# Starting every on-chip tile of a fp32 two-block network on a multiple of 64 or 128 bytes

## The chip, the core and the metric

The kernel runs on one core of a Trainium2 chip. The metric is the device time of one execution in microseconds. The kernel is timed several times and the median counts; the profile is one further execution, recorded by the hardware profiler.

## What is computed

The reference is a network on 256 tokens of 1024 features, all in fp32. Its first block adds to the input a pair of linear-attention mixers (RWKV-7 and GLA) and then a mixture of 32 experts, two of them for each token. Its second block has two layers, each made of a feed-forward half, a mixer (two attentions and a Fourier branch, each gated) and another feed-forward half, with scales and shifts that come from a condition vector; it takes the output of the first block as one stream of tokens and a given context as another. Cut to what matters here:

```
x = x + concat(rwkv7(rmsnorm(x) @ w_in), gla(...)) @ w_out        # block 1
x = x + sum over 2 of 32 experts of (silu(h @ w_gate) * (h @ w_up)) @ w_down
for each of 2 layers:                                             # block 2, x and context
    x = x + 0.5 * gate * ffn(rmsnorm(x) * scale + shift)
    x = x + gate * mixer(rmsnorm(x) * scale + shift, keys of the context)
    x = x + 0.5 * gate * ffn(rmsnorm(x) * scale + shift)
```

Nearly all of the arithmetic is products of a weight matrix with the 256 tokens.

## The kernel before

Features lie on the 128 partitions of the on-chip memory (SBUF) and the 256 tokens lie along a partition, so one row of a tile of tokens is 256 fp32 numbers, 1024 bytes. A weight comes in chunks of eight 128x128 tiles. A chunk goes through four steps. SyncE issues a DMA of 128x1024 numbers into one of eight buffers named `raw` (or into further ones, named `room`, while they exist; line 313). ScalarE rounds it to the format that TensorE multiplies in one pass, into `whi` (line 319). VectorE subtracts that from the chunk, into `wlo` (line 320). TensorE then makes three matmuls for each 128x128 tile, in `mm3`: `whi` by the tokens' high part (line 334), `whi` by the tokens' low part (line 335), and `wlo` by the tokens' high part (line 336). Each loads 128x128 weights and moves 128x256 numbers of tokens past them. The next three for the same output add to the same bank of PSUM.

The tokens' operands are pairs of tiles, too. `norm_split` (line 453) writes `hnh` and `hnl`: for each of the 8 groups of 128 features VectorE scales x into a small tile `hnt` of which there are two (line 463), ScalarE adds the shift and rounds into `hnh` (line 468), and VectorE takes the difference into `hnl` (line 469). The feed-forward's inner values are `h0` and `h1` (lines 328 and 329), the branches' are `yh` and `yl`. In some norms the operand is made before the norm is known; then it is `xs0` and `xs1`, rows of 256 numbers and 2 more for the shift (lines 373 to 377).

The letter at the end of a name is the chain that the tile belongs to. Chain x is block 1's mixers and runs until about 447 us. Chain c is the context's way through block 2; it runs from there to 1640 us, with the experts of block 1 (tiles that end in m, products `bm`) between its matmuls. Chain z is the main tokens' way through block 2; it has the chip to itself from 1712 us to the end. The chains' tiles lie at different addresses: long-lived tiles at the left end of a partition, the chains' own ones packed from the right end or behind the left ones.

The order of the work on TensorE and SyncE is written out by the emitting code: generators yield steps, and `_run`, `_zip` and `_merge` choose by an internal clock which goes next. VectorE, ScalarE and GpSimd are ordered by the scheduler of the tile layer, which follows buffers as they come free. The tile layer packs tiles at multiples of 32 bytes.

Of the kernel before, what the change touches and what calls it, by code (L numbers as in the profile page):

```python
# [10 lines left out]
F32 = mybir.dt.float32  # L11
# [8 lines left out]
T = 256  # L20
# [5 lines left out]
HD = 64  # L26


# ----------------------------------------------------------------- host layout
def _tiles(w, cols):  # L30
    """[K, n] -> column tiles in the order of `cols` (lists of 128 column indices), each as K/128 tiles."""
    K = w.shape[0]
    return [w[k * 128:(k + 1) * 128, c] for c in cols for k in range(K // 128)]


def _chunks(tiles):
    """List of [128, 128] tiles -> [n / 16, 128, 16 * 128], zero filled."""
    n = -(-len(tiles) // 16) * 16
    a = np.zeros((n, 128, 128), np.float32)
    for i, t in enumerate(tiles):  # L40
        a[i, :, :t.shape[1]] = t
    return np.ascontiguousarray(a.reshape(n // 16, 16, 128, 128).transpose(0, 2, 1, 3).reshape(n // 16, 128, 2048))


def _cols(v):
    """[n] -> [128, n / 128]."""
    return np.asarray(v, np.float32).reshape(-1, 128).T
# [153 lines left out]
# ----------------------------------------------------------------- the chip's program  # L201
class _Chain:
    """What a chain of the program works with: its tiles in SBUF and its banks of PSUM."""
# [9 lines left out]
    def hold(self):  # L213
        """A bank that stays while others come and go; two at a time."""
        return self.ps.tile([128, 512], F32, tag="h" + self.name, name="h" + self.name, bufs=2)
# [4 lines left out]
    @contextmanager  # L220
    def scope(self, name):
        """A chain whose tiles last as long as the scope."""
        with self.pool(name=name + self.name, bufs=1) as sb:
            yield self.sub(sb)
# [6 lines left out]
class _Net:  # L231
# [7 lines left out]
    def open(self, cpool, rpool, nraw):  # L239
# [8 lines left out]
        self.selT = cpool.tile([128, 512], F32R, name="selT")  # L248

    def splits(self, ch, pool, n):  # L250
        """The pool that holds the split weights of the chain from here on, and its buffers."""
# [37 lines left out]
    # -- weights  # L289
    def arrival(self):  # L290
        """When the next weights would be there, by the clock of the emission."""
# [4 lines left out]
    def room(self, pool, n):  # L296
        """More room for weights that are on their way."""
# [28 lines left out]
    def split_act(self, hi, lo, src):  # L326
        """hi + lo = src, for operands of matrix products."""
# [3 lines left out]
    def mm3(self, out, w, x, first, last, **kw):  # L331
        """out += w.T @ x with both split."""
# [5 lines left out]
    # -- small arithmetic  # L338
    def rsqrt(self, ch, ms, n, eps, tag="rs", op=OP.add):
        """1 / sqrt(ms + eps) on [128, n], in SBUF; with op max, 1 / sqrt(max(ms, eps))."""  # L340
# [13 lines left out]
    def sumsq(self, ch, x, k, nxt=None, eng=None):  # L354
        """Adds the squares of x, the k-th of KD, to the chain's sums: one of all but the last, and the last. With
        nxt, the scale and shift that the norm takes, x by the scale is split ahead of it, the shift beside it."""
# [15 lines left out]
        if k == 0:  # L372
            top.xs = [top.tile([128, KD, T + 2], f"xs{i}", F32R) for i in range(2)]
            self.split_act(*(t[:, :, T:] for t in top.xs), shift[:, :, None].to_broadcast([128, KD, 2]))
# [4 lines left out]
    def early(self, ch, xs, w, tiles, banks):  # L379
        """Products of the first tiles of a weight with what the norm hasn't scaled yet, its shift's beside it."""  # L380
        for o in tiles:
            b = ch.bank()
            banks.append(b)
            for k in range(KD):
                self.mm3(b[:, :T + 2], w.get(o + k), (xs[0][:, k], xs[1][:, k]), k == 0, k == KD - 1)
# [3 lines left out]
    def norm_early(self, ch, x, scale, shift, w, tiles):  # L389
        """norm_split, and what early gives meanwhile: banks, that times the rows of 1 / rms are products, up to a  # L390
        shift by feature in their column T."""
# [10 lines left out]
    def scaled(self, ch, b, rs):  # L402
        """A bank of norm_early times rs, and its shift, in SBUF."""
# [5 lines left out]
    def rstd(self, ch, x, w1=0.7, w2=2.2):  # L409
        """x [128, KD, T], features on partitions: 1 / rms over the features, on all partitions, [128, T] in PSUM."""  # L410
# [5 lines left out]
    def rstd_cols(self, ch, x, w1=0.7, w2=2.2):  # L416
        """1 / rms of the tokens of x, [128 tokens, 2]."""
# [25 lines left out]
    def spread(self, ch, y):  # L443
        """[128 tokens, 2] -> the value of each token on all partitions, [128, T] in PSUM."""
# [8 lines left out]
    def norm_split(self, ch, x, scale, shift, rs=None):  # L453
        """rms norm of x, times scale, plus shift, as split operands [128, KD, T]; 1 / rms into rs."""
# [6 lines left out]
        for k in range(KD):  # L461
            t = ch.tile([128, T], "hnt", bufs=2)
# [11 lines left out]
    # -- block 1  # L474
    def rows(self, b, j, x, n):
        """Means over the heads of x, tile j of n, into the bank b (with unrows)."""
        self.nc.tensor.matmul(b[32 * j:32 * j + 32, :T], self.c("sel")[:, :32], x, start=True, stop=True)

    def parted(self, ch, rs):
        """Values by row as operands of unrows: the high parts in 8 rows of 32, the low parts in the next 8."""  # L480
# [6 lines left out]
    def unrows(self, out, j, st, n=0):  # L487
        """The rows of st for tile j + 4 n on the partitions of its heads."""
# [3 lines left out]
    def head_rsqrt(self, ch, sqs, eps, op):  # L492
        """1 / rms over the heads of 4 tiles, from their squares: [8 heads' high parts, 8 low parts; T], by head_rows."""
# [22 lines left out]
    def mixers(self, ch):  # L516
        """RWKV-7 and GLA of the norm of the input; the input plus their output projection into self.x."""
# [93 lines left out]
    def rwkv(self, ch, sh, lora, yg):  # L611
# [3 lines left out]
        left = self.tc.tile_pool  # L615
# [41 lines left out]
    def until(self, n):  # L657
        """Waits for the mixers of block 1 to have come to their n-th stage."""
# [3 lines left out]
    def beside(self, ch, sh, lora, yg, wo, x, bonus, gate):  # L662
        """What the solve of RWKV-7 doesn't give: its bonus and gate, in place of v and r, and GLA's output projection."""
# [191 lines left out]
    def blocks_out(self, lq, n):  # L855
        """The 32 x 32 blocks on the diagonals of one direction, to where they come back from a block to a partition."""
# [4 lines left out]
    def invert(self, k, ld, kk):  # L861
        """Inverses of the blocks on the diagonals, a block in each partition; in the room of k, ld and kk."""
# [22 lines left out]
    def solve(self, ch, tt, lu, lq, xab, xx):  # L885
        """The solve of RWKV-7 by triangles of 32 x 32; what it gives is added to the latter half of self.x."""
# [5 lines left out]
        def out(j, g):  # L892
            """The part of the output that comes from the first or second 128 tokens to be solved."""
# [14 lines left out]
        def correct(g, corr, todo):  # L908
            """What triangles of u add to those of the m-th after them."""
# [8 lines left out]
        def right(g):  # L918
            """Banks with the right sides of the first or second 128 tokens to be solved."""
# [59 lines left out]
    def rwkv_out(self, ch, bonus, gate, yh, yl):  # L979
        """The group norm of RWKV-7's output, its bonus and its gate, as split operands."""  # L980
# [138 lines left out]
    def route(self, ch, x):  # L1119
        """The router's choices for the tokens of x, and its norm by token (scaled once the tokens have partitions)."""  # L1120
# [46 lines left out]
        def first_max(f, n):  # L1167
            """The index of the first maximum over the last axis, and the maximum."""
# [63 lines left out]
        # assignments beyond an expert's 32 slots go to blocks of 32 of their own  # L1232
# [45 lines left out]
    def swiglu_rows(self, ch, bg, bu, n):  # L1278
        """silu(gate) * up of n rows of 512, and its transpose [128, 4, n]."""
# [14 lines left out]
    def moe(self, ch, x, load, loads):  # L1294
        """x += experts; 4 experts of 32 slots at a time."""
# [69 lines left out]
    def moe_over(self, ch_of, x):  # L1365
        """x += what the assignments beyond 32 of an expert add, a block of 32 of them at a time."""
# [58 lines left out]
    # -- block 2  # L1425
    def silu_c(self, ch):
        """silu of both conditions as stationary operands [128, KD, 32] (columns 0, 1; zeros beyond)."""
# [3 lines left out]
        for m, name in enumerate(("c", "c_ctx")):  # L1431
            t = ch.tile([128, KD], "silc", bufs=2)
            u = ch.tile([128, KD], "silu", bufs=2)
# [4 lines left out]
    def ada(self, ch, l):  # L1438
        """Modulation vectors of layer l: {0: for x, 1: for ctx} -> [128, 72], and what the norms take of them."""
# [4 lines left out]
        m2 = [self.cp.tile([128, 72], F32, name=f"mod{l}{m}") for m in range(2)]  # L1444
# [25 lines left out]
        for m in range(2):  # L1470
            mm = m2[m].rearrange("p (n k) -> p n k", k=KD)
            a = self.cp.tile([128, 3, KD], F32, name=f"nsc{l}{m}")
# [3 lines left out]
            g = self.cp.tile([128, 3, KD], F32, name=f"gsc{l}{m}")  # L1476
# [6 lines left out]
    def lam(self, ch, l):  # L1483
        """-lambda of layer l on all partitions, [128, 1]."""
        nc = self.nc
        lv = self.v(f"lam{l}")
        p = ch.tile([128, 2], "lamp")
# [3 lines left out]
        e = ch.tile([128, 2], "lame")  # L1491
        nc.scalar.activation(e, b[:, :2], AF.Exp)
        qg = self.cp.tile([128, 4], F32, name=f"qkg{l}")
# [3 lines left out]
        nl = self.cp.tile([128, 1], F32, name=f"nlam{l}")  # L1497
        li = 0.8 - 0.6 * math.exp(-0.3 * l)
        nc.vector.scalar_tensor_tensor(nl, e[:, 1:2], li, e[:, 0:1], op0=OP.subtract, op1=OP.subtract)
        gs = self.cp.tile([128, 1], F32, name=f"subg{l}")  # L1500
# [79 lines left out]
    def project(self, ch, hn, l, rope, y, w, first, full=True):  # L1580
        """Queries, keys and values of the tokens, and the operands of the Fourier branch into y."""
# [77 lines left out]
    def rotate(self, ch, qk, norm, rs, l, rope):  # L1659
        """The norm of queries and keys, and their rotation."""  # L1660
# [21 lines left out]
    def fourier(self, ch, uc, y):  # L1682
        """The operands of the Fourier branch into y."""
# [20 lines left out]
    def attend(self, ch, kind, q, keys, y, l=None, room=None):  # L1704
        """Attention of the queries q on the keys, a pair of heads (kind a) or of maps (kind b) at a time, into y. With
        room, a pair of [128, KD, T] tiles, queries and keys are split there."""
# [11 lines left out]
        def prepare(j):  # L1718
            """The operands of the scores of pair j: the queries', and each keys'."""
# [106 lines left out]
    def mixer(self, ch, x, mod, l, rope, other=None, keep=None, full=True, nxt=None):  # L1826
        """The mixer of block 2: `other` gives keys of other tokens, ahead of the own ones; `keep` stores the own."""
# [8 lines left out]
        with ch.scope("macc") if full else nullcontext(ch) as ca:  # L1836
            acc = ca.tile([128, KD, T], "macc") if full else None
            with ch.scope("mix") as cm:
# [6 lines left out]
                if full:  # L1845
                    keys = keys + [r]
                    room = None if first is None else [ch.top.tile([128, KD, T + 2], f"xs{i}", F32R) for i in range(2)]
# [23 lines left out]
    def gate(self, b, hn, wb, o):  # L1871
        """The gate of a branch into the first half of the bank b, its weights from the o-th tile on."""
# [5 lines left out]
    def gates(self, ch, hn, wb, th):  # L1878
        """tanh of half the last branch's first gates."""
# [293 lines left out]
```

## Time and profile before

| | us |
|---|---|
| median of 3 runs | 2986.49 (2985.42 to 2990.33) |
| span of the profiled execution, first to last instruction | 2977.6 |
| TensorE busy in it | 2856.5 (96%) |
| VectorE busy | 1781.8 (60%) |
| ScalarE busy | 1235.6 (41%) |
| GpSimd busy | 179.3 (6%) |
| mean busy share of the 16 DMA engines in 40 slices | between 0.2 and 0.9 |

For the profiled execution the trace gives its span alone; the runs lie 7.8 to 12.7 us above it, which is what lies before the first and after the last recorded instruction. In the rows a matmul of 128x256 numbers shows some 0.28 us from its start to its end, although the next one starts about 0.12 us after it: matmuls follow each other through a pipeline. The speed of a stream of matmuls is therefore read from the distance between starts and not from the busy time. PE means TensorE, PEld its loading of weights, DVE VectorE, ACT ScalarE, POOL GpSimd and SP SyncE.

### The profile page before, as it was taken

What the parts mean: (1) busy time and instruction counts of PE and PEld (TensorE: products, weight loads), DVE (VectorE), ACT (ScalarE), POOL (GpSimd) and SP (SyncE); (2) the same over time, 40 slices, a digit from 0 to 9 for tenths busy, and PEclk for the clock granted to TensorE, in tenths of its full rate; (3) what the DMA queues carried; (4) which work ended last, traced back from release to release, by engine and by line L of the source; (5) the groups of instructions that cost most, each with busy time, mean ns of one, the idle gap of its engine ahead of it and who ended that gap; (6) DMA issues with size and microseconds to landing.
All of it is one profiled execution on the core that took longest, in us unless ns stands there. A gap on an engine that the chain in (4) does not pass through costs nothing. (4 is left out here: it accounts for less than half of the span.)

```text
span 2977.6 us, 55032 instructions
## 1 busy us (share of the span) xinstructions
PE 2856.5 (96%) x22394; PEld 2419.8 (81%) x22394; DVE 1781.8 (60%) x3517; ACT 1235.6 (41%) x2071; POOL 179.3 (6%) x207
## 2 busy tenths in 40 slices
PE   8999777999999999999999899999999999999999
PEld 5756457787756778877887699989999999899999
DVE  4565565454534454545545766767776767766865
ACT  3321133333324333333333454556554545465543
POOL 0110110000000010000000000010200000101100
PEclk9999888999999999999999999999999999999999
DMA  8755857887787888897988565523556556424564
GB/s 316 251 177 176 292 212 197 299 290 280 235 274 271 303 281 317 291 339 285 336 294 312 183 197 193 192 82 107 163 191 196 181 196 201 139 86 137 169 194 132
DMA packets 198897, 667.47 MB, mean 224 GB/s; under 512 B 36850, under 2 KB 37874, under 8 KB 198002
## 3 DMA queue, kind: packets, MB, share of 16 engines
q1 hardware_dynamic: 180144, 656.04, 63.8%
q10 hardware_dynamic: 18498, 7.90, 1.3%
q8 instruction: 176, 2.88, 0.4%
q14 instruction: 79, 0.65, 0.1%
HBM read 658.05 MB, written 5.80 MB: 223 GB/s over the span
## 5 line engine op out<-in xcount | busy, mean ns | idle before, releaser
L320 DVE TENSOR_TENSOR wlo<-raw,whi 128x1024 fp32r<-128x1024 f32 x623 | 767.7, 1233 | 493.9 <-ACT whi L319 481.4
L319 ACT CAST whi<-raw 128x1024 fp32r<-128x1024 f32 x631 | 661.6, 1050 | 772.4 <-issue 278.6
L334 PE MATMUL bz<-hnhz,whi 128*128 128x256 f32 x1920 | 539.8, 281 | 0.7 <-ACT hnhz L328 0.7
L335 PE MATMUL bz<-hnlz,whi 128*128 128x256 f32 x1920 | 532.7, 277 | 4.2 <-DVE hnlz L329 4.2
L336 PE MATMUL bz<-hnhz,wlo 128*128 128x256 f32 x1920 | 532.0, 277 | 0.6 <-DVE wlo L320 0.6
L334 PE MATMUL bc<-hnhc,whi 128*128 128x256 f32 x1504 | 440.6, 293 | 13.0 <-ACT whi L319 12.2
L335 PE MATMUL bc<-hnlc,whi 128*128 128x256 f32 x1504 | 428.5, 285 | 4.8 <-DVE hnlc L469 2.8
L336 PE MATMUL bc<-hnhc,wlo 128*128 128x256 f32 x1504 | 427.7, 284 | 4.8 <-DVE wlo L320 4.8
L334 PEld LDWEIGHTS bz<-hnhz,whi 128*128 128x128 f32 x1920 | 361.4, 188 | 9.6 <-issue 5.7
L334 PEld LDWEIGHTS bc<-hnhc,whi 128*128 128x128 f32 x1504 | 289.6, 193 | 94.0 <-issue 37.2
L335 PEld LDWEIGHTS bz<-hnlz,whi 128*128 128x128 f32 x1920 | 361.4, 188 | 5.5 <-DVE hnlz L329 5.4
L336 PEld LDWEIGHTS bz<-hnhz,wlo 128*128 128x128 f32 x1920 | 361.5, 188 | 0.8 <-DVE wlo L320 0.8
L335 PEld LDWEIGHTS bc<-hnlc,whi 128*128 128x128 f32 x1504 | 290.1, 193 | 7.5 <-DVE hnlc L469 5.9
L336 PEld LDWEIGHTS bc<-hnhc,wlo 128*128 128x128 f32 x1504 | 289.7, 193 | 6.4 <-DVE wlo L320 6.4
L334 PE MATMUL bz<-h0z,whi 128*128 128x256 f32 x704 | 194.3, 276 | 0.0
L335 PE MATMUL bz<-h1z,whi 128*128 128x256 f32 x704 | 194.3, 276 | 0.0
L336 PE MATMUL bz<-h0z,wlo 128*128 128x256 f32 x704 | 194.3, 276 | 0.0
L334 PE MATMUL bc<-h0c,whi 128*128 128x256 f32 x528 | 154.2, 292 | 0.6 <-ACT h0c L328 0.6
L335 PE MATMUL bc<-h1c,whi 128*128 128x256 f32 x528 | 150.1, 284 | 0.9 <-DVE h1c L329 0.9
L336 PE MATMUL bc<-h0c,wlo 128*128 128x256 f32 x528 | 149.8, 284 | 0.0
L1337 PE MATMUL bm<-raw,mxm 128*32 128x512 f32 x752 | 147.3, 606 | 1.1 <-DMA raw<-moe_gu 1.1
L320 DVE TENSOR_TENSOR wlo<-room,whi 128x1024 fp32r<-128x1024 f32 x75 | 91.7, 1224 | 86.9 <-ACT whi L319 77.8
(702 smaller groups left out, 5328.1 us busy)
## 6 DMA issues: line engine op xcount, KB each, us to landing
raw<-wi SPq DMA_DIRECT2D x263, 512.0 KB, 4.7
raw<-moe_gu SPq DMA_DIRECT2D x188, 512.0 KB, 7.1
raw<-wada SPq DMA_DIRECT2D x144, 512.0 KB, 4.8
raw<-wo SPq DMA_DIRECT2D x124, 512.0 KB, 4.5
raw<-wbr SPq DMA_DIRECT2D x108, 512.0 KB, 3.7
raw<-win SPq DMA_DIRECT2D x104, 512.0 KB, 5.0
raw<-moe_dn SPq DMA_DIRECT2D x103, 512.0 KB, 5.9
room<-moe_gu SPq DMA_DIRECT2D x68, 512.0 KB, 8.9
```

Of the source, the lines that this page charges most:

```text
L319: self.nc.scalar.copy(hi, src)
L320: eng.tensor_tensor(lo, src, hi.bitcast(F32), op=OP.subtract)
L334: mm(out, w[0], x[0], start=first, stop=False, **kw)
L335: mm(out, w[0], x[1], start=False, stop=False, **kw)
L336: mm(out, w[1], x[0], start=False, stop=last, **kw)
L1337: mm(b[32 * j:32 * j + 32], xt[:, k, 32 * j:32 * j + 32], r[:, j % 2 * 512:j % 2 * 512 + 512], start=(k == 0), stop=(k == KD - 1))
```

## The change

A wrapper, `_Pool`, stands between the kernel and the pools of SBUF. It rounds the size of each tile up, to 16 numbers (64 bytes) if it has no more than 16 on a partition and otherwise to a multiple of 32 numbers (128 bytes), and hands out the first part of it. Pools of PSUM and of DRAM are as before. The many small vectors (modulation, its derived scales, and the like) become slices of one tile, `small`. The rows of `xs0` and `xs1` become 272 numbers (1088 bytes) where they were 258 (1032 bytes). A tile of 96 bytes, `edge`, is put at the right end of the partition so that what is packed from there begins on a multiple of 128. `norm_split`'s temporary comes from the chain's general pool `w` (three buffers) and no longer from `hnt` (two). The rest of the difference takes away comments.

```diff
+XS = T + 16
+class _Pool:
+    def tile(self, shape, dt=F32, **kw):
+        n = math.prod(shape[1:])
+        full = 16 if n <= 16 else -(-n // 32) * 32
+        if full == n:
+            return self.pool.tile(shape, dt, **kw)
+        t = self.pool.tile([shape[0], full], dt, **kw)[:, :n]
+        if len(shape) == 2:
+            return t
+        names = "abcd"[:len(shape) - 1]
+        return t.rearrange(f"p ({' '.join(names)}) -> p {' '.join(names)}", **dict(zip(names, shape[1:])))
+def _pools(tc):
+    @contextmanager
+    def pool(name, bufs=1, **kw):
+        with tc.tile_pool(name=name, bufs=bufs, **kw) as p:
+            yield p if "space" in kw else _Pool(p)
+    return pool
...
+        self.small, self.taken = cpool.tile([128, 544], F32, name="small"), 0
+    def take(self, n):
+        self.taken += n
+        return self.small[:, self.taken - n:self.taken]
...
-            top.xs = [top.tile([128, KD, T + 2], f"xs{i}", F32R) for i in range(2)]
-            self.split_act(*(t[:, :, T:] for t in top.xs), shift[:, :, None].to_broadcast([128, KD, 2]))
+            top.xs = [top.tile([128, KD, XS], f"xs{i}", F32R) for i in range(2)]
+            self.split_act(*(t[:, :, T:T + 2] for t in top.xs), shift[:, :, None].to_broadcast([128, KD, 2]))
...
-                self.mm3(b[:, :T + 2], w.get(o + k), (xs[0][:, k], xs[1][:, k]), k == 0, k == KD - 1)
+                self.mm3(b[:, :T + 2], w.get(o + k), (xs[0][:, k, :T + 2], xs[1][:, k, :T + 2]), k == 0, k == KD - 1)
...
         for k in range(KD):
-            t = ch.tile([128, T], "hnt", bufs=2)
+            t = ch.tile([128, T], "w", bufs=ch.nw)
...
-        left = self.tc.tile_pool
+        left = _pools(self.tc)
...
-        m2 = [self.cp.tile([128, 72], F32, name=f"mod{l}{m}") for m in range(2)]
+        m2 = [self.take(72) for m in range(2)]
...
-            a = self.cp.tile([128, 3, KD], F32, name=f"nsc{l}{m}")
+            a = self.take(3 * KD).rearrange("p (i k) -> p i k", i=3)
...
-    pool = tc.tile_pool
+    pool = _pools(tc)
...
+    ctx.enter_context(tc.tile_pool(name="edge", bufs=1, side="right")).tile([128, 24], F32, name="edge")
     rp = ctx.enter_context(pool(name="raw", bufs=1))
     net.open(base, rp, 8)
+    net.cw, net.nover = net.take(4), net.take(1)[0:1].bitcast(I32)
```

Where the tiles start, in both programs as they are built: the remainder of the byte address in a partition by 128 (a second buffer of the same tile, or the next row, is a multiple of 128 further on, but for the rows of xs).

| tile | before | after |
|---|---|---|
| raw | 32 | 0 |
| whi, wlo (all chains) | 32 | 0 |
| hnhx, hnhc, h0c | 32 | 0 |
| hnhz, h0z | 96 | 0 |
| yhz | 0 | 64 |
| xs0z, first row and further ones | 96, then 8 more each | 0 or 64 |
| mstm, mxm (experts' sums) | 64 | 64 |
| mylm (experts' sums) | 96 | 0 |
| x | 0 | 0 |

TensorE and SyncE run the same instructions in the same order before and after, under other names. ScalarE, VectorE and GpSimd change places at the norms. On ScalarE, at the second norm of chain z (`hnhz` is the normalised tokens' high part, `hntz` and `wz` the temporary, `mod` and `small` the shift), before:

```order
L458 COPY hnrz<-bz 128x256
L319 CAST whi<-raw 128x1024 x2
L468 ACTIVATE hnhz<-hntz,mod_325 128x256 x2
L319 CAST whi<-raw 128x1024
L468 ACTIVATE hnhz<-hntz,mod_325 128x256 x2
L319 CAST whi<-raw 128x1024
```

and after, where lines 353, 492 and 502 are the former lines 319, 458 and 468:

```order
L492 COPY hnrz<-bz 128x256
L353 CAST whi<-raw 128x1024 x2
L502 ACTIVATE hnhz<-wz,small 128x256 x3
L353 CAST whi<-raw 128x1024
L502 ACTIVATE hnhz<-wz,small 128x256 x3
L353 CAST whi<-raw 128x1024
```

The eight activations come in groups of three instead of two between the casts of the weights, with a cast less among them. On VectorE at the same norm, before:

```order
L320 TENSOR_TENSOR wlo<-raw,whi 128x1024
L463 SCALAR_TENSOR_TENSOR hntz<-x,nsc_2509,bz 128x256 x2
L320 TENSOR_TENSOR wlo<-raw,whi 128x1024
L469 SCALAR_TENSOR_TENSOR hnlz<-hntz,mod_325,hnhz 128x256 x2
L463 SCALAR_TENSOR_TENSOR hntz<-x,nsc_2509,bz 128x256 x2
L320 TENSOR_TENSOR wlo<-raw,whi 128x1024
```

and after, where lines 354, 497 and 503 are the former lines 320, 463 and 469:

```order
L354 TENSOR_TENSOR wlo<-raw,whi 128x1024
L497 SCALAR_TENSOR_TENSOR wz<-x,small,bz 128x256 x3
L354 TENSOR_TENSOR wlo<-raw,whi 128x1024
L503 SCALAR_TENSOR_TENSOR hnlz<-wz,small,hnhz 128x256 x3
L497 SCALAR_TENSOR_TENSOR wz<-x,small,bz 128x256 x3
L503 SCALAR_TENSOR_TENSOR hnlz<-wz,small,hnhz 128x256 x3
L497 SCALAR_TENSOR_TENSOR wz<-x,small,bz 128x256 x2
```

Here, too, three of a kind stand together, and fewer subtractions for the weights come between them.

## Rows read from the trace of the kernel before

**Rows 1.** The page's part on the engines: busy time, share, instructions.

```profile
PE 2856.5 (96%) x22394; PEld 2419.8 (81%) x22394; DVE 1781.8 (60%) x3517; ACT 1235.6 (41%) x2071; POOL 179.3 (6%) x207
```

**Rows 2.** Stretches: length; PE, PEld, DVE, ACT, POOL busy (count); clock; DMA share; GB/s.

```profile
471.60:474.60 3.00, 3.00 (x16) 3.00 (x15) 2.76 (x21) 1.34 (x4) 0.00 (x0) 0.50 0.76 287
520.00:1640.00 1120.00, 1095.74 (x8285) 867.44 (x8284) 555.74 (x943) 406.98 (x649) 37.83 (x40) 1.00 0.82 294
1265.48:1339.90 74.42, 73.63 (x584) 58.45 (x583) 34.63 (x46) 27.71 (x39) 2.17 (x3) 1.00 0.90 339
1712.00:2977.60 1265.60, 1242.82 (x10369) 1195.80 (x10367) 877.01 (x1512) 650.22 (x1076) 83.79 (x88) 1.00 0.50 162
```

**Rows 3.** Groups by line: busy us, mean ns of one, idle before and what ended it.

```profile
L320 DVE TENSOR_TENSOR wlo<-raw,whi 128x1024 fp32r<-128x1024 f32 x623 | 767.7, 1233 | 493.9 <-ACT whi L319 481.4
L319 ACT CAST whi<-raw 128x1024 fp32r<-128x1024 f32 x631 | 661.6, 1050 | 772.4 <-issue 278.6
L334 PE MATMUL bz<-hnhz,whi 128*128 128x256 f32 x1920 | 539.8, 281 | 0.7 <-ACT hnhz L328 0.7
L334 PE MATMUL bc<-hnhc,whi 128*128 128x256 f32 x1504 | 440.6, 293 | 13.0 <-ACT whi L319 12.2
...
L334 PE MATMUL bz<-h0z,whi 128*128 128x256 f32 x704 | 194.3, 276 | 0.0
...
L334 PE MATMUL bc<-h0c,whi 128*128 128x256 f32 x528 | 154.2, 292 | 0.6 <-ACT h0c L328 0.6
```

**Rows 4.** Timeline of PE, chain z, 195 matmuls without a break (first, last).

```profile
2240.05 0.28 PE L335 MATMUL bz<-hnlz,whi 128*128 128x256 f32 x1
...
2262.03 0.28 PE L334 MATMUL bz<-hnhz,whi 128*128 128x256 f32 x1
```

**Rows 5.** Timeline of PE, chain c, 65 matmuls without a break (first, last).

```profile
591.35 0.28 PE L335 MATMUL bc<-h1c,whi 128*128 128x256 f32 x1
...
599.02 0.28 PE L336 MATMUL bc<-h0c,wlo 128*128 128x256 f32 x1
```

**Rows 6.** Timeline of PE, chain c at half clock, 12 matmuls (first, last).

```profile
472.12 0.42 PE L336 MATMUL bc<-hnhc,wlo 128*128 128x256 f32 x1
...
474.47 0.41 PE L335 MATMUL bc<-hnlc,whi 128*128 128x256 f32 x1
```

**Rows 7.** Line 793, plain fp32 matmuls: eight in a row, and their durations.

```profile
201.12 1.99 PE L793 MATMUL bx<-arx,bkx 64*128 64x256 f32 x8
...
L793 PE MATMUL bx<-arx,bkx x128: 376/376/480, 192.2 to 274.7; 64*128 64x256 f32 x128
```

**Rows 8.** Timeline of PE: 15 matmuls of mstm, 11 of yhz/ylz (first, last).

```profile
952.27 0.28 PE L1360 MATMUL bm<-mstm,mylm 128*128 128x256 f32 x1
...
953.90 0.28 PE L1360 MATMUL bm<-mstm,mylm 128*128 128x256 f32 x1
...
2022.15 0.28 PE L335 MATMUL bz<-ylz,whi 128*128 128x256 f32 x1
...
2023.33 0.28 PE L336 MATMUL bz<-yhz,wlo 128*128 128x256 f32 x1
```

**Rows 9.** Groups by line, the norms' operations of chains c and z.

```profile
L334 PE MATMUL bz<-xs0z,whi 128*128 128x258 f32 x288 | 82.5, 286 | 0.7 <-ACT vac L1656 0.7
...
L468 ACT ACTIVATE hnhz<-hntz,mod 128x256 fp32r<-128x256 f32 x48 | 21.8, 501 | 3.0 <-DVE hntz L463 3.0
...
L468 ACT ACTIVATE hnhc<-hntc,mod 128x256 fp32r<-128x256 f32 x40 | 18.3, 501 | 35.0 <-DVE hntc L463 34.9
```

**Rows 10.** The page's DMA issues: KB each, us to landing.

```profile
raw<-wi SPq DMA_DIRECT2D x263, 512.0 KB, 4.7
...
x<-x_T SPq DMA_DIRECT2D x2, 512.0 KB, 5.3
```

**Rows 11.** DVE's groups: the same subtraction of 128x256 numbers, chains z and c.

```profile
L329 DVE TENSOR_TENSOR h1z<-wz,h0z 128x256 fp32r<-128x256 f32 x76 | 31.8, 419 | 0.0
L329 DVE TENSOR_TENSOR h1c<-wc,h0c 128x256 fp32r<-128x256 f32 x66 | 27.9, 422 | 21.2 <-ACT h0c L328 21.2
```

More of the change, by code (lines that the diff above doesn't have):

```diff
@@ L198, in _consts, with __init__ @@
     return dict(const=main, selT=selT, const1=np.ascontiguousarray(np.concatenate(c, 1)), const2=rest), (off0, off, off2)
+class _Pool:
+    def __init__(self, pool):
+        self.pool = pool
+    def tile(self, shape, dt=F32, **kw):
[14 more added lines that the diff above has]
+    return pool
 class _Chain:
@@ L1431, in silu_c @@
         for m, name in enumerate(("c", "c_ctx")):
-            t = ch.tile([128, KD], "silc", bufs=2)
-            u = ch.tile([128, KD], "silu", bufs=2)
+            t = self.take(KD)
+            u = self.take(KD)
             nc.scalar.activation(t, self.v(name), AF.Tanh, scale=0.5)
@@ L1475, in ada @@
                                                op0=OP.add, op1=OP.mult)
-            g = self.cp.tile([128, 3, KD], F32, name=f"gsc{l}{m}")
+            g = self.take(3 * KD).rearrange("p (i k) -> p i k", i=3)
             for i in range(3):
@@ L1486, in lam @@
         lv = self.v(f"lam{l}")
-        p = ch.tile([128, 2], "lamp")
+        p = self.take(2)
         nc.vector.tensor_tensor(p, lv[:, 0:4:2], lv[:, 1:4:2], op=OP.mult)
@@ L1490, in lam @@
         nc.tensor.matmul(b[:, :2], self.ones, p, start=True, stop=True)
-        e = ch.tile([128, 2], "lame")
+        e = self.take(2)
         nc.scalar.activation(e, b[:, :2], AF.Exp)
-        qg = self.cp.tile([128, 4], F32, name=f"qkg{l}")
+        qg = self.take(4)
         for i in range(4):
@@ L1496, in lam @@
         self.qkg[l] = [qg[:, i:i + 1] for i in range(4)]
-        nl = self.cp.tile([128, 1], F32, name=f"nlam{l}")
+        nl = self.take(1)
         li = 0.8 - 0.6 * math.exp(-0.3 * l)
         nc.vector.scalar_tensor_tensor(nl, e[:, 1:2], li, e[:, 0:1], op0=OP.subtract, op1=OP.subtract)
-        gs = self.cp.tile([128, 1], F32, name=f"subg{l}")
+        gs = self.take(1)
         nc.vector.tensor_scalar(gs, self.v(f"subln{l}"), 1.0 - li, None, op0=OP.mult)
@@ L1846, in mixer @@
                     keys = keys + [r]
-                    room = None if first is None else [ch.top.tile([128, KD, T + 2], f"xs{i}", F32R) for i in range(2)]
+                    room = None if first is None else [ch.top.tile([128, KD, XS], f"xs{i}", F32R) for i in range(2)]
                     wb = self.stream(ch, f"wbr{l}")
@@ L2048, in tile_net @@
     net.x = base.tile([128, KD, T], F32, name="x")
-    net.cw = base.tile([128, 4], F32, name="cw")
-    net.nover = base.tile([1, 1], I32, name="nover")
     def keep(l, r):
```

## The prediction

> **What bounds the kernel now.** I read the engines' busy times first, then the stretches, the groups by line, and last the timeline of PE in quiet places, because the groups' durations can't tell a stream's speed.
>
> PE is busy for 2856.5 us, 96% of the span, and no other engine passes 60% [rows 1]. In chain z, from 1712 us to the end, PE is busy for 1242.8 of 1265.6 us while the DMA engines are busy for 0.50 of the time [rows 2]. In chain c PE is busy for 1095.7 of 1120 us, and here the DMA engines come to 0.82, in the slice from 1265 us to 0.90 [rows 2]. ScalarE's cast takes 1050 ns and VectorE's subtraction 1233 ns for a chunk that gives PE 24 matmuls [rows 3], some 2.7 us at 113 ns each, so both engines keep up. The three chains' ends are set by how fast PE issues, and only a change of the distance between matmuls can move the time by more than a little.
>
> That distance is what the timeline shows. In chain z 195 matmuls start in 21.98 us, 194 steps of 113.3 ns [rows 4]. In chain c 65 start in 7.67 us, 64 steps of 119.8 ns [rows 5]. [...] I take 106.7 + 2.4 = 109.1 ns as the pace of a stream that isn't held up.
>
> The two chains run the same code on the same kind of operands, and the program gives them different addresses: weights at 32 past a multiple of 128 in both, tokens at 32 in chain c and at 96 in chain z. They differ in the load of the DMA engines too; the change alters the addresses.
>
> **The change part by part.**
>
> *Alignment of the matmuls' operands.* Afterwards nearly all of them start on a multiple of 128. Chain z has 3 x (1920 + 704) matmuls of hnhz and h0z [rows 3] and 3 x 288 of xs0z [rows 9], 8736 in all. If each falls from 113.3 to 109.1, that is 4.2 ns x 8736 = 37 us; to 106.7 it would be 6.6 x 8736 = 58 us. Chain c has 3 x (1504 + 528) = 6096 [rows 3]. From 119.8 to 109.1 is 10.7 x 6096 = 65 us, to 106.7 it is 80 us, and to the 113.3 of chain z 40 us.
>
> I don't take all of it, because two rows speak against a full cure. Tokens that already start on a multiple of 64 (yhz at 0, mstm at 64) aren't fast: 10 steps of yhz and ylz take 1.18 us, 118 ns, and 14 steps of mstm, which alternates with weights at 64 and at 96, take 1.63 us, 116.4 ns [rows 8]. These are short runs behind a stall, and the weights of the first are still at 32, so they bound but don't decide. [...] For chain z I take half, 18 us. In chain c PE would then ask for weights sooner. With 43 us less the stretch of 1120 us has its DMA share go from 0.82 to 0.82 x 1120 / 1077 = 0.85, and the slice at 0.90 has little left. I take two thirds of 65, 43 us. Chain x has few such matmuls and other limits; I count nothing.
>
> What the trace of before can't show is a stream with both operands on multiples of 128 in long runs. From below it is bounded by 138 us of gain (58 + 80). From above, by the worst pace that the rows show for chain z, 119.8: a loss of 6.5 x 7872 = 51 us.
>
> [...]
>
> *Alignment for the other engines.* VectorE's subtraction of 128x256 numbers takes 419 ns in chain z, where its tiles are at 96, and 422 in chain c at 32 [rows 11]. I cost it at nothing; both engines have idle time (the 493.9 and 772.4 us ahead of their main groups, [rows 3]) to hide a few per cent either way.
>
> *Alignment for the DMAs.* The input's transfers go to a tile at 0 and take 5.3 us for 512 KB; those of raw, at 32, take 4.7 [rows 10]. No gain of alignment is seen, and the queues are not the same at both times. I cost it at nothing. PE's lead hides it in chain z.
>
> *The norms.* With three buffers instead of two, VectorE gets a step further ahead of ScalarE. ScalarE's waits for hnt are 35.0 us over chain c and 3.0 over chain z [rows 9], but PE waited for hnhz 0.7 us in all [rows 3], because the emission puts other matmuls there. Against it, a cast of weights now stands behind three activations of 501 ns instead of two, 0.5 us later at each of 11 norms (88 rows of eight). At worst all of that reaches PE, 11 x 2 x 0.5 = 11 us; at best a good part of the 13.0 us that PE waited for the casts at hnhc [rows 3] goes. I take 2 us of gain.
>
> *One tile for the small vectors.* Slices of one tile may add waits where there were separate tiles. The instruction that would wait is a norm's first, on VectorE, with the weights' subtractions queued behind it. All such vectors are written early in block 1 and read much later. I take 3 us of loss, with 0 and 10 as ends.
>
> *Sum.* 18 + 43 + 2 - 3 = 60 us off the span of 2977.6, 2917.6. The runs' median of 2986.49 lies 8.9 above the span, so the time is 2926 us.
>
> **The rivals.**
>
> *Nothing happens.* The excess may come of something that goes with the chains but not with alignment, such as the DMA load, 0.82 in the one and 0.50 in the other [rows 2]. For it: yhz, with its tokens at 0, is not quick. Against it: the excess is the same for 194 matmuls in a row, while the other engines come and go. The time is 2986, with 6 us to both sides for the norms and the small tile.
>
> *Distance decides, and chain z becomes like chain c.* Perhaps it is not where a row starts that matters but where tokens and weights lie to each other: in chain c both are at 32, a distance of 0, and the pace is the worst; in chain z the distance is 64, and the pace is better. The change puts all operands of chain z at 0 too. Its steps would go from 113.3 to 119.8: 6.5 x 7872 = 51 us more. Chain c stays as it is. The time is 2986 + 51 = 3037. [...] Against it: both operands of chain c are off a multiple of 64, so the trace has no case with distance 0 and aligned rows in a long run. It decides if the first long run of hnhz in chain z shows steps over 117 ns; if chain c gains 6.5 ns at the same time, the two cancel within 11 us.
>
> *Chain c meets its DMAs.* If chain c's matmuls fall to 109.1 but the transfers hold the stretch at a DMA share of about 0.90, it can shrink to 1120 x 0.82 / 0.90 = 1020 us at most, 100 us, more than the 65 asked. This bounds nothing on the mean; in slices that stand at 0.90 already it takes the gain away. With a third of it lost I have it in the sum; with all of it lost the time is 2969.
>
> **How the numbers follow.** Aligned rows gain in at least one chain and the other doesn't lose as much: 0.55, with times from 2850 to 2970, the likeliest 2926 (the case with the DMAs, 0.06, lies in it). Nothing happens: 0.19, from 2980 to 2992. Chain z becomes like chain c: 0.23, from 2995 to 3040 according to what chain c does meanwhile. The remaining 0.03 go to waits of the norms and of the small tile, to the slow side. Runs of the kernel before differ by 4.9 us, 0.16%, so less than 0.2%, 6 us, can't be told from no change. Faster has the 0.55 and a little of the second case, 0.57; the same is 0.17; slower 0.26. The range runs from 2860, where nine tenths of the alignment's largest gain are in, to 3020, which leaves out the last part of the third case, about 0.13, and a few per cent below. The likeliest case's own range is 2860 to 2970.
>
> **What the profile after would show.** Right: in chain z long runs of hnhz with steps of 109 to 112 ns; in chain c steps of 109 to 114 ns; the stretch of chain z some 18 us shorter and that of chain c some 43, with a higher DMA share. The groups of VectorE and ScalarE keep their durations of 419, 501, 1050 and 1233 ns. Waits at the norms stay within a few us of before. Wrong: steps of 113.3 and 119.8 in the same places (the first rival's view), or steps near 120 in chain z with the same activity beside them (the second's). It would also be wrong if chain c's steps fell but its stretch didn't, with the queue of transfers waiting for nothing and PE waiting for casts behind DMAs.

## The result, and the profile after

The changed kernel takes 3031.32 us (median of 4 runs, 3026.66 to 3037.41) where the kernel before takes 2988.41 in the same measurement. The ratio is 1.0149, 95% interval 1.0131 to 1.0168: 43 us slower, where I forecast 60 us faster, and 11 us beyond the range.

The profiled execution is the slowest of the four. Its span is 3035.6 us, 58.0 more than before. Part of that is the choice of the two executions: in every run with both on record 1.7 or 1.8 us lie outside the span (3037.41 and 3035.6 here), so the profiled execution of the kernel before, with its span of 2977.6, was some 9 us quicker than its median. The 8.9 us that the forecast adds to that span are mostly this, and not time outside the recorded instructions. The first row is the page's part on the engines; then come three stretches, with the columns of [rows 2].

```profile
PE 2912.2 (96%) x22394; PEld 2469.1 (81%) x22394; DVE 1779.0 (59%) x3517; ACT 1233.9 (41%) x2071; POOL 180.1 (6%) x207
...
340.00:400.00 60.00, 57.36 (x782) 35.24 (x776) 14.77 (x40) 8.53 (x14) 2.35 (x1) 0.84 0.65 227
520.00:1640.00 1120.00, 1089.74 (x8245) 864.45 (x8247) 552.41 (x931) 405.06 (x644) 37.80 (x40) 0.99 0.82 294
1725.20:3035.60 1310.40, 1284.90 (x10369) 1235.86 (x10367) 875.08 (x1510) 648.16 (x1073) 84.01 (x88) 1.00 0.47 156
```

PE's busy time grew by 56 us, the others' stayed [rows 1]. Chain z took 1265.6 us [rows 2] and takes 1310.4 for the same 10369 matmuls: 44.8 us, all of the measured difference. It needs fewer transfers at a time now, 0.47 against 0.50, so it isn't they that hold it. The other 13 us of this span lie between 340 and 520 us, where PE's granted clock was 0.50 of the full one for longer in this execution (from 360 to 368 us, for one; the mean is 0.84 in the slice shown). Before, the same slice had 0.98:

```profile
340.00:400.00 60.00, 57.36 (x881) 35.20 (x879) 17.03 (x43) 9.70 (x16) 2.36 (x1) 0.98 0.75 260
```

The four runs' mean clocks go from 0.976 in the profiled one to 0.982 in the quickest, and the medians lie 43 us apart, so most of this part belongs to the two executions that were profiled. Whether the change has some share in it isn't shown: matmul by matmul, the five other profiles of kernels built on the changed one (below) take 4 to 11 us more for this stretch than the kernel before (this one 15), and the three built on the kernel before 2 to 3 us.

The timeline of PE shows what chain z does. The first fence is a stretch of hnhz in the changed kernel, 195 matmuls without a break (first, last); the second has the groups by line, with the columns of [rows 3].

```profile
1749.77 0.28 PE L369 MATMUL bz<-hnlz,whi 128*128 128x256 f32 x1
...
1772.79 0.28 PE L368 MATMUL bz<-hnhz,whi 128*128 128x256 f32 x1
```

```profile
L353 ACT CAST whi<-raw 128x1024 fp32r<-128x1024 f32 x631 | 660.2, 1047 | 825.9 <-issue 343.4
...
L368 PE MATMUL bc<-hnhc,whi 128*128 128x256 f32 x1504 | 441.3, 293 | 12.5 <-ACT whi L353 11.6
...
L368 PE MATMUL bz<-h0z,whi 128*128 128x256 f32 x704 | 198.1, 281 | 0.0
```

194 steps in 23.02 us are 118.7 ns; before they were 113.3 [rows 4]. The group h0z shows the same as 281 against 276 ns. Chain c's groups have not moved, 293 ns as before [rows 3], though everything in it now starts on a multiple of 128. 5.4 ns by the 7872 matmuls of hnhz and h0z would be 43 us. So alignment did nothing for chain c and something made chain z worse.

The rest is as it was. The fence has groups of VectorE and ScalarE, and a row of the DMA issues.

```profile
L363 DVE TENSOR_TENSOR h1z<-wz,h0z 128x256 fp32r<-128x256 f32 x76 | 31.8, 418 | 0.0
L363 DVE TENSOR_TENSOR h1c<-wc,h0c 128x256 fp32r<-128x256 f32 x66 | 27.9, 423 | 21.2 <-ACT h0c L362 21.2
...
L502 ACT ACTIVATE hnhc<-wc,small 128x256 fp32r<-128x256 f32 x40 | 17.7, 500 | 26.6 <-DVE wc L497 26.5
...
raw<-wi SPq DMA_DIRECT2D x263, 512.0 KB, 4.6
```

The cast takes 1047 ns (1050 in [rows 3]), the subtractions 418 and 423 (419 and 422 in [rows 11]), the norm's activation 500 (501 in [rows 9]), a transfer to raw 4.6 us (4.7 in [rows 10]). ScalarE's waits for the temporary of the norms fell from 35.0 us [rows 9] to 26.6 over chain c.

### The profile page after: what moved, and what is told of

Its sections match the earlier page's. It is cut to its first block, busy times and chain, and to the rows that moved or that the text cites. A ratio compares the mean times of both kernels' runs of the same rounds, so it can differ in the third digit from the quotient of the medians.

```text
span 3035.6 us, 55059 instructions
## 1 busy us (share of the span) xinstructions
PE 2912.2 (96%) x22394; PEld 2469.1 (81%) x22394; DVE 1779.0 (59%) x3517; ACT 1233.9 (41%) x2071; POOL 180.1 (6%) x207
## 5 line engine op out<-in xcount | busy, mean ns | idle before, releaser
L353 ACT CAST whi<-raw 128x1024 fp32r<-128x1024 f32 x631 | 660.2, 1047 | 825.9 <-issue 343.4
L368 PE MATMUL bz<-hnhz,whi 128*128 128x256 f32 x1920 | 550.1, 287 | 0.6 <-ACT hnhz L362 0.6
L369 PE MATMUL bz<-hnlz,whi 128*128 128x256 f32 x1920 | 543.1, 283 | 4.3 <-DVE hnlz L363 4.3
L370 PE MATMUL bz<-hnhz,wlo 128*128 128x256 f32 x1920 | 542.6, 283 | 0.0
L1489 PE MATMUL ba<-raw,cond 128*32 128x512 f32 (+1 forms) x640 | 138.9, 613 | 5.4 <-DMA raw<-wada 5.4
```

The source lines that it names most:

```text
L353: self.nc.scalar.copy(hi, src)
L368: mm(out, w[0], x[0], start=first, stop=False, **kw)
L369: mm(out, w[0], x[1], start=False, stop=False, **kw)
L370: mm(out, w[1], x[0], start=False, stop=last, **kw)
L1489: nc.tensor.matmul(b[32 * j:32 * j + 32, :nb], self.cond[:, k], r[:, o:o + nb], start=(k == 0), stop=(k == KD - 1))
```

## Experiments

In this section the *distance* of a stream of matmuls is the address of its tokens less that of its weights, by 256 bytes. By the addresses of both programs as they are built it was 0 in chain c and 192 in chain z (hnh and h0) before the change; after it 0 and 128.

**A map of distances (m1_map).** The kernel holds nothing but streams of the three matmuls, one after another, with tiles at chosen places:

```diff
+for w in (0, 32):
+    for x in (0, 32, 64, 96, 128, 160, 192, 224):
+        b = stream(w, x)      # 144 matmuls: whi by xhi, whi by xlo, wlo by xhi
```

> Not the network: a stream of fp32r matmuls alone (three for each 128x128 tile, 128x256 tokens, 144 in a row for each pair), weights at 0 or 32 bytes past a multiple of 256 (w0, w32), tokens at 0, 32, ... 224 past one (x0 to x224); the output isn't computed. Theory 1 (the distance between tokens and weights decides): w0 with x_d and w32 with x_(d+32) show the same step, worst at a distance of 0 (119.8 ns, as chain c), 113.3 ns at a distance of 192 (as chain z before) and some 118.7 at 128 (as chain z after). Theory 2 (the start of each row decides): the steps go by the tokens' own place, so x64 gives the same with w0 and with w32, and the multiples of 64 differ from the others. Theory 3 (other engines and DMAs at work beside PE make the excess): all pairs show one step, 109 ns or less, since nothing else runs here.

The rows are the groups of the first matmul of the three (48 or 64 of it; between them lie the other two), with the least, median and largest duration in ns and the first and last start.

```profile
L60 PE MATMUL b<-x32h,w0h x48: 280/280/284, 52.3 to 68.9; 128*128 128x256 f32 x48
L60 PE MATMUL b<-x128h,w0h x48: 279/281/285, 103.5 to 120.2; 128*128 128x256 f32 x48
L60 PE MATMUL b<-x192h,w0h x48: 276/276/279, 137.5 to 153.5; 128*128 128x256 f32 x48
L60 PE MATMUL b<-x32h,w32h x48: 280/283/283, 187.9 to 204.8; 128*128 128x256 f32 x48
L60 PE MATMUL b<-x160h,w32h x48: 279/281/285, 256.3 to 273.1; 128*128 128x256 f32 x48
L60 PE MATMUL b<-x224h,w32h x64: 276/276/279, 290.3 to 311.8; 128*128 128x256 f32 x64
```

From the first to the last start lie 141 steps (189 for the 64). The tokens at 32 take 16.6 us with weights at 0, 117.7 ns a step, and 16.9 us with weights at 32, 119.9. At a distance of 192 the step is 113.5 and 113.8 to the digit of these rows, at 128 it is 118.4 and 119.1, whichever multiple the tiles start on. With the weights at 0 or at 32, the place of a row by itself changes nothing; the pace goes with its distance to the weights. That holds with DMAs, VectorE and ScalarE idle, so theory 3 falls as well. Averaged over the steps of a stream in the trace (the first 20 left out):

| distance | 0 | 32 | 64 | 96 | 128 | 160 | 192 | 224 |
|---|---|---|---|---|---|---|---|---|
| ns, weights at 0 | 120.0 | 117.8 | 117.8 | 120.0 | 118.7 | 117.4 | 113.3 | 118.3 |
| ns, weights at 32 | 120.0 | 117.8 | 117.8 | 120.0 | 118.7 | 117.4 | 113.3 | 118.3 |

The same places came a second time at the end, in the reverse order. There 64 ran at 113.3 and 192, with weights at 0, at 117.8: these two distances have more than one steady pace, and they share the two, 113.3 and 117.8.

**The finer map (m2_fine).** Weights at 0, tokens at every 8 bytes.

> Not the network: the same stream of matmuls alone, weights at 0, tokens at every 8 bytes from 0 to 248 (every 4 from 180 to 208), again in the reverse order, and at 256 to 480 in steps of 32; the output isn't computed. Theory 1 (distance by 256): the steps of 256 + d are those of d, 113.3 ns stand around 192 and nowhere fall to 106.7. Rival (a finer or a longer period): some place off a multiple of 32 is quicker than 113.3, or 256 + d differs from d.

Nothing is quicker than 113.3 ns, which stands at 64, 112 and 192; on the way up 8, 24, 72 and 184 give 120 or more. 256 + d gives what d can give: 120.0 at 256, 118.7 at 384, 113.3 at 448 (192). At 192 the pace depended on what ran ahead, and other distances changed theirs in the reverse order too (120 from 122.2 to 120.0, 144 from 118.7 to 116.7). Of the quick places 112 alone ran at 113.3 in both orders; it was not tried in the network. The fence shows matmuls in the middle of two such streams, 94 of line 85 and 51 of line 108 (first, last).

```profile
368.27 0.28 PE L85 MATMUL b<-xl,wh 128*128 128x256 f32 x1
...
378.81 0.28 PE L85 MATMUL b<-xl,wh 128*128 128x256 f32 x1
...
656.08 0.28 PE L108 MATMUL b<-xl,wh 128*128 128x256 f32 x1
...
661.96 0.28 PE L108 MATMUL b<-xh,wh 128*128 128x256 f32 x1
```

Both have their tokens at 192. The first, after a stream at 184, makes 93 steps in 10.54 us, 113.3 ns; the second, after one at 200, 50 steps in 5.88 us, 117.6 by these digits and 117.8 in the trace. Each keeps its pace to its end. In the same way 64 ran at 113.3 after 56 and at 117.8 after 72.

**Chain z at other distances (b_right64, a_right64).** The kernel before with chain z moved to a distance of 128, and the changed one with chain z at 64:

```diff
 # b_right64, on the kernel before
+    ctx.enter_context(right(name="edge", bufs=1)).tile([128, 16], F32, name="edge")
 # a_right64, on the changed kernel
-    ...tile([128, 24], F32, name="edge")
+    ...tile([128, 40], F32, name="edge")
```

> The kernel before with 64 bytes at the right end: nothing is aligned, weights at 32 and chain z's tokens at 160, the distance of 128 that the changed kernel has. Theory 1: chain z's steps rise from 113.3 to 118.7 ns and the time to about 3030 us without anything of the change. Theory 2: tokens and weights are off a multiple of 64 by 32 as before; 113.3 ns and 2987 us.

> The changed kernel with a further 64 bytes at the right end, so that chain z's tokens stand 64 past a multiple of 256 and the weights at 0: all on multiples of 64, at a distance of 64. Theory 1: chain z's steps fall from 118.7 to some 113 ns, and the time comes down by some 40 us to about 2988. Theory 2: tokens on a multiple of 64 stay as they are, 118.7 ns, or get slower for being off a multiple of 128; 3030 us.

b_right64 takes 3020.99 us, ratio to the kernel before 1.0118 (95% interval 1.0090 to 1.0146; so the intervals below). A gap of 64 bytes, with nothing aligned and nothing else of the change, gives most of the slowdown: in its profile chain z takes 41 us more than before for the same matmuls, where the changed kernel's takes 44.8. Its timeline, 194 matmuls of hnhz:

```profile
1749.94 0.28 PE L336 MATMUL bz<-hnhz,wlo 128*128 128x256 f32 x1
...
1772.85 0.28 PE L334 MATMUL bz<-hnhz,whi 128*128 128x256 f32 x1
```

193 steps in 22.91 us, 118.7 ns. a_right64 takes 3021.54 us, 1.0119 (1.0095 to 1.0142), and not the 2988 expected. The same stretch of its timeline, 195 matmuls:

```profile
1749.95 0.28 PE L369 MATMUL bz<-hnlz,whi 128*128 128x256 f32 x1
...
1772.80 0.28 PE L368 MATMUL bz<-hnhz,whi 128*128 128x256 f32 x1
```

194 steps in 22.85 us are 117.8 ns, the slower pace of a distance of 64. That alone doesn't refute the period of 128 bytes, which the second rival had assumed, since 64 and 192 share their two paces. The map does: 0 and 128 step at 120.0 and 118.7 ns, 96 and 224 at 120.0 and 118.3.

**Chain c at 64 and at 192 (a_c64, a_c192).**

```diff
+                es.enter_context(tc.tile_pool(name="k0", bufs=1)).tile([128, 48], F32, name="k0")   # a_c64: 16
                 ch = _Chain("c", es.enter_context(pool(name="k1", bufs=1)), ca.ps, pool)
```

> The changed kernel with 64 bytes ahead of chain c's tiles: its tokens at 64, weights at 0; chain z as in the changed kernel. Theory 1: chain c's steps fall from 119.8 to some 113 ns, 6.5 ns by 6096 matmuls, 40 us less if the transfers follow: about 2990 us. Theory 2: 119.8 ns in chain c, 3030 us.

> The changed kernel with 192 bytes ahead of chain c's tiles: its tokens 192 past its weights; chain z as in the changed kernel. Theory 1: chain c's steps fall from 119.8 to 113.3 ns; by 6.5 ns x 6096 the time falls by 40 us to about 2990. Rival (the transfers hold chain c at a DMA share of 0.8 to 0.9): the steps fall, but half or more of the 40 us comes back as waits for weights; 3010 or more.

a_c64 takes 3012.06 us, 1.0090 (1.0067 to 1.0114), by the ratios 18 us less than the changed kernel; its steps are mostly 117.8 where 113 were expected, and 12 of the 18 us lie in chain c. a_c192 takes 2997.93 us, 1.0046 (1.0029 to 1.0063), 31 less. Its stretch, and the 65 matmuls of [rows 5] in it (first, last):

```profile
520.00:1640.00 1120.00, 1087.13 (x8446) 855.68 (x8446) 577.74 (x985) 419.65 (x673) 37.73 (x40) 0.99 0.82 299
...
597.61 0.28 PE L369 MATMUL bc<-h1c,whi 128*128 128x256 f32 x1
...
604.88 0.28 PE L370 MATMUL bc<-h0c,wlo 128*128 128x256 f32 x1
```

The 64 steps take 7.27 us, 113.6 ns, where they were 119.8 [rows 5]. In the same 1120 us it does 8446 matmuls where the changed kernel does 8245, at the same DMA share: the transfers don't take the gain. Most streams of chain c run at 113.3 to 113.8, some at 117.8 (its mean over runs of hnhc is 114.5). That is 5.3 ns less than 119.8, 32 us over 6096 matmuls, and matmul by matmul chain c is 32 us shorter than in the changed kernel.

**Chain z back at 192 (a_z192), and with the rows of xs as before (a_z192_rows).**

```diff
 # a_z192, on the changed kernel
-    ...tile([128, 24], F32, name="edge")
+    ...tile([128, 8], F32, name="edge")
 # a_z192_rows, further
-XS = T + 16
+XS = T + 2
-        full = 16 if n <= 16 else -(-n // 32) * 32
+        full = n if n == KD * XS else 16 if n <= 16 else -(-n // 32) * 32
+            top.tile([128, 32], "gap")      # so that xs0 and xs1 stand at 64 and 128
             top.xs = [top.tile([128, KD, XS], f"xs{i}", F32R) for i in range(2)]
```

> The changed kernel with 64 bytes less at the right end: everything still on multiples of 64, and chain z's tokens 192 bytes past its weights by 256, as before the change. Theory 1: chain z's steps are 113.3 ns again and the time falls by 45 us to that of the kernel before, 2986. Rival (the other parts of the change, the norms' third buffer and the shared small tile, cost as well): it stays some 10 us above.

a_z192 takes 3017.66 us, 1.0119 (1.0097 to 1.0140), 35 above the kernel before in the same measurement (2982.90). Theory 1 as I had put it missed. The timeline of the stream of hnhz that follows xs (195 matmuls, first and last):

```profile
1749.83 0.28 PE L370 MATMUL bz<-hnhz,wlo 128*128 128x256 f32 x1
...
1772.68 0.28 PE L369 MATMUL bz<-hnlz,whi 128*128 128x256 f32 x1
```

194 steps in 22.85 us are 117.8 ns at a distance of 192. The streams that start after a real stall ran at 113.3 in the same execution; those that follow xs without one ran at 117.8 through all of hnhz (912 matmuls) and the 528 of h0z behind it. (Two short ones behind other matmuls without a stall, at 2107 and 2765 us, ran at 117.8 too, as the same two did in the kernel before.) In the kernel before, hnhz behind xs ran at 113.3 throughout. What differs ahead of it are the rows of xs: 1032 bytes apart before, 1088 in the changed kernel, and so other distances in the last matmuls.

> The changed kernel with chain z's tokens 192 past its weights and, in addition, the rows of xs0 and xs1 as before the change: 1032 bytes apart, the first at distances of 64 and 128. Everything else of the change stays. Theory A (at a distance of 192 a stream has two steady paces, 113.3 and 117.8 ns, and keeps the one into which the matmuls of xs ahead of it have led it; rows of 1088 bytes lead into the slow one): the streams of hnhz and h0z behind xs run at 113.3 again and the time falls from 3018 to that of the kernel before, 2983 to 2988. Theory B (something else of the change, the norms or the shared tile, made a_z192 slow): 3018 as there.

a_z192_rows takes 2984.97 us; the kernel before takes 2985.76 on the same chip, ratio 0.9996 (0.9981 to 1.0011). The timeline of its h0z, 195 matmuls:

```profile
1819.91 0.28 PE L370 MATMUL bz<-h0z,wlo 128*128 128x256 f32 x1
...
1841.89 0.28 PE L369 MATMUL bz<-h1z,whi 128*128 128x256 f32 x1
```

194 steps in 21.98 us, 113.3 ns. Theory A holds, though the first place of the rows and the space between them were put back together, so which of the two decides isn't shown. This kernel has the multiples of 64 or 128 for all but xs, the shared small tile and the norm's three buffers, and it is as quick as before: these parts together are worth nothing within 0.2%.

**A kernel that beats both (b_c192, best).** The one line of a_c192 in the kernel before, and with chain x set 192 apart as well:

```diff
+                es.enter_context(tc.tile_pool(name="k0", bufs=1)).tile([128, 48], F32, name="k0")
 # best, further
+            cp.tile([128, 16], "gap")
+                co.tile([128, 16], "gap")
```

> The kernel before with 192 bytes ahead of chain c's tiles and nothing else: chain c's tokens 192 past its weights, chain z untouched. Theory (distance): chain c's steps fall from 119.8 to 114 ns as in a_c192, where the time fell by 33 us: some 2950 us. Rival (the gain in a_c192 was a matter of that kernel): 2984.

> b_c192 with chain x's weights and tokens set 192 apart too (64 bytes of gap in each of two of its pools). Chain x has some 600 such matmuls, 119.6 to 113.3 ns: 4 us less than b_c192 if PE decides there, nothing if its transfers do: 2946 to 2950.

b_c192 takes 2956.11 us, 0.9893 (0.9874 to 0.9913); best takes 2951.89, 0.9892 (0.9873 to 0.9910). The gap ahead of chain c gives 30 us. The stretch of chain c in b_c192:

```profile
520.00:1640.00 1120.00, 1095.48 (x8445) 861.45 (x8445) 575.19 (x975) 415.84 (x662) 37.74 (x40) 0.99 0.81 297
```

These are 8445 matmuls where the kernel before does 8285 [rows 2]. Chain x's gap gives nothing that can be told. Against the changed kernel's ratio of 1.0149, b_c192 is 2.5% quicker.

## Why the prediction was wrong, by its steps

*What bounds the kernel: right.* PE's steps set the time in chain z, and in chain c a_c192 got what its steps promised. Apart from the stretch at the lower clock, nothing else in the trace moved by more than 5 us. The pace goes with the operands and not with the other engines or the DMAs: in m1_map it runs from 113.3 to 120.0 ns by their places while all else is idle.

*"If each falls from 113.3 to 109.1", "For chain z I take half, 18 us": wrong, with its sign.* It rose to 118.7, 44.8 us over the chain. The step that failed is the one before: that a multiple of 64 or 128 is what a row needs. m1_map gives 120.0 ns with both operands at 0 and 113.3 with both off every multiple of 64 (x224, w32). 109.1 isn't reached at any of the distances tried. No run shows the 106.7 and 2.4 ns that it is added up from, so the 18 and 43 us rest on figures that weren't measured, and so does the largest gain of 138 us (58 + 80), which set the quick end of the range. What the runs showed in their place is 113.3 ns as the pace of the quickest long streams of 128x256 matmuls, 194 steps in 21.98 us [rows 4].

*"I take two thirds of 65, 43 us" in chain c: wrong.* It had a distance of 0 before and has it after, and 119.8 ns at both. The term was there to be had, by another edit: a_c192 got 31 us with a distance of 192, and with no loss to the transfers, which I had feared.

*The evidence that I weighed too lightly.* Both rows that I named against a full cure were cases of distance. yhz at 0 stood at 224 from its weights, which m1_map gives as 118.3; the row showed 118 [rows 8]. mstm stood at 0 and 224 in turn, 120.0 and 118.3; its 116.4 [rows 8] is below both, and not for being a short run: from the second on its steps of 114 to 119 ns repeat after every six, and six of the seven such runs in the trace lie at 116.6 to 116.8. Two distances in turn have a pace of their own, which no map tried. Neither start on a multiple of 64 had helped, and I put that on the weights.

*The second rival: right in kind.* It had distance as the cause, chain z going to 119.8, and 3037 us. Its period of 128 bytes is refuted by m1_map; by 256, 128 is a place of its own with 118.7. That chain z would lose 51 us was close to the 44.8, in part by luck, since it took the pace of 0 for that of 128. What it lacked is the second pace at one distance, by which the rows of xs decide over the stream behind them: at a distance of 192 but with the new rows (a_z192) chain z still takes 30 us more than before.

*The small terms.* The norms (2 us of gain), the small tile (3 of loss), the other engines and the DMAs (nothing): together nothing within 0.2%, by a_z192_rows. They aren't nothing each. In the four profiles that have the change and leave chain c at a distance of 0 (the changed kernel, a_right64, a_z192, a_z192_rows) the 8425 matmuls from 520 to 1665 us of the kernel before take 4.5 to 7.2 us less than there, and the 243 from there to 1712 us 4.5 to 4.7 more; b_right64, without the change, shows 0.6 and 0.1. Which part does it isn't shown.

What stays open is the mechanism inside: the runs show that the pace goes with the distance of the tokens from the weights by 256 bytes (m1_map: 120.0 ns at 0, 118.7 at 128, 113.3 at 192) and at 64 and 192 also with what ran before (113.3 or 117.8), not why. They don't show either why chain c's step of 213.6 ns at a granted clock of 0.50 [rows 6] isn't halved at 1.00: half would be 106.8, an estimate, and the rows have 119.8 [rows 5]. Nor do the runs give a rule for which of the two paces a stream takes on; for the rows of xs it was found by trying.

## What to carry to other kernels

Where streams of the same matmul step at different paces, as 113.3 and 119.8 ns here, look at where its two operands lie to each other before rounding addresses: try gaps of 32 or 64 bytes ahead of one of them and read the distance between starts in the timeline. A quick layout can be luck that an unrelated edit undoes, so note the pace of each long stream and compare it after every change that moves tiles. A map of the places in a kernel of its own costs one run; this one, with 120.0 ns at 0, 118.7 at 128 and 113.3 at 192, would have told which way this change goes.

## What the runs showed of the hardware

Matmuls of 128x256 numbers in fp32r, each with its own weights, step at 113.3 to 122.2 ns by the tokens' distance from the weights (m2_fine, mean granted clock 0.999), and at a distance of 192 at 113.3 or 117.8 by what ran before. At a granted clock of 0.50 the rows show one distance, 0, with 213.6 ns [rows 6], 1.78 times the 119.8 of chain c at 1.00 [rows 5]. The plain fp32 matmuls of 64x256 numbers in [rows 7], at 1.00, make one step of 320 ns and then six of 215.7 in the trace.
